# Tiles of a feed-forward group's second product placed between the next group's units

## The chip, the cores and the metric

The kernel runs on one core of a Trainium2 chip. Its engines work side by side, each through its own list of instructions: TensorE (PE; its weight loads are shown as PEld), VectorE (DVE), ScalarE (ACT), GpSimd (POOL) and SyncE (SP), which here issues the DMAs. The metric is the time of one execution on the device in microseconds (us), from several runs.

## What is computed

An encoder block of two layers on 512 tokens of width 1024. Each layer is feed-forward, token mixing, feed-forward, and a gated projection of a side input ("ple"), each followed by a layer norm. The change is in the feed-forward stage, of which there are four in all:

```python
D_MODEL, D_FF = 1024, 2816

def swiglu(x, w_in, w_out):
    gate, up = jnp.split(x @ w_in, 2, axis=-1)
    return (jax.nn.silu(gate) * up) @ w_out

x = layer_norm(ALPHA * x + 0.5 * swiglu(x, ffn_w_in[i, 0], ffn_w_out[i, 0]), ln_g[i, 0], ln_b[i, 0])
```

Inputs and weights are float32. The kernel works to more than half precision by writing each operand as a sum of two float16 numbers, `hi` and `lo`, and multiplying hi x hi, hi x lo and lo x hi: three matmuls for one (`mm3`, lines 253 to 258).

## The kernel before

The middle width of 2816 is cut into 22 columns of 128, numbered m = 0 to 21 (`MF` = 22). Column m of the gate and of the up half makes a **unit**: first product, silu, gating, and the result `h` for column m, stored as hi and lo in a tile `hT` that holds a pair of columns (`hT[m // 2]`, lines 279 to 287).

Units 0 and 1 are computed directly (lines 291 to 346). Units 2 to 21 use a Strassen-like scheme with seven products instead of eight: `load_quad` (line 430) loads two blocks of 512 KB of the first weight into a tile `f`, splits the two raw slots into hi and lo (ACT line 139, DVE line 140), and, in `rest`, makes four sums on DVE (line 453) and splits them as well, into slots 0 to 6 of a tile `wq` in the pool `ring` (three buffers; `f` has two). `begin(m)` (line 375) runs slot 0 into a PSUM bank `pA` and slot 4 into `pB`. `step(new, old)` (line 386) is a software pipeline over two units: slot 5 of the old unit, slot 2 of the new, slot 3 of the old, then silu and gating of the old, slot 1 of the new (bank `pC`), slot 6 of the new, and the copy `up` (lines 407 and 408). Each slot is twelve matmuls of 256 columns, so a unit is 84.

The second weight comes in pairs of rows: `load_rows` (line 156) loads 1 MB for columns k and k + 1 into one of three `raw` buffers and splits it (two halves on ACT line 139, two on DVE line 140) into a tile `w` of the pool `w2`, which has four buffers. `w2` also holds the weights of units 0 and 1, and the constants of the layer norm (`ln_gb`, line 169).

The columns are worked off in four **groups**, `groups = [(0, 4), (4, 10), (10, 16), (16, 22)]` (line 267), called groups 0 to 3 here. For each group (lines 410 to 428) the units run, `step(None, unit)` empties the pipeline, the group's two or three pairs of `w_out` are taken, and four **tiles** of 128 tokens follow: `out_proj` (line 459) multiplies `hT` by `w`, twice 512 output columns, each in a bank `po`, and adds them to `x` in SBUF (DVE line 472). A tile is 24 matmuls of 512 columns for group 0 and 36 for the others. In the last group each tile is followed by its layer norm.

```python
            for gi, (m0, m1) in enumerate(groups):
                unit = None
                for m in range(max(m0, 2), m1):
                    following = begin(m)
                    step(following, unit)
                    fetch(1)
                    unit = following
                step(None, unit)
                wo = weights((m1 - m0) // 2)
```

`loads` (lines 305 to 310) is the order in which weights are asked for: a group's quads, then its row pairs. `fetch(n)` keeps n of them issued ahead, `weights(n)` takes the next n.

PSUM: `acc` (line 58) hands out two banks, shared by `pC` and `po`; `bank` and `bank2` three each, for `pA` and `pB`. SBUF pools opened inside the stage (`hT`, `ring`, `f`) are given back at its end, and the next stage's pools lie on the same bytes; with `reuse_waits="tile"` a new tile waits for the old tiles that it lies on.

The order in which each engine gets its instructions isn't the order of the code alone: when the program is built, a list scheduler goes through the instructions by priority (their place in the code) and gives an engine that is free, by its estimate, the first one that is ready. At run time each engine keeps to that order and waits on semaphores.

Of the kernel before, what the change touches and what calls it, by code (L numbers as in the profile page):

```python
# [13 lines left out]
ALU = mybir.AluOpType  # L14
# [7 lines left out]
NT = S // P  # L22
DFF = 2816
MF = DFF // P
DEPTH = 2
ALPHA = (2 * DEPTH) ** 0.25
# [4 lines left out]
IWS = 1.0 / WS  # L31


class Block:
# [225 lines left out]
    def ffn(self, i, f, j, last=False):  # L260
        nc = self.nc
        w_in, w_out = self.ins["ffn_w_in"][i, f], self.ins["ffn_w_out"][i, f]
        xT, x = self.xT, self.x
# [3 lines left out]
        groups = [(0, 4), (4, 10), (10, 16), (16, MF)]  # L267
        with ExitStack() as ctx:
            pool = lambda name, bufs: ctx.enter_context(
                self.tc.tile_pool(name=name, bufs=bufs, reuse_waits="tile")  # L270
            )
            hpool = pool("hT", 4)
            self.ring = pool("ring", 3)
            self.fpool = pool("f", 2)
            hT = {}

            def gated(m, sg, ups, scale):

                if m % 2 == 0:
                    hT[m // 2] = hpool.tile([P, 2, 2, S], F16, name="hT")  # L280
                for u, part in ups:
                    nc.vector.scalar_tensor_tensor(
                        part(sg), u, scale, part(sg), op0=ALU.mult, op1=ALU.mult
                    )
                hi, lo = hT[m // 2][:, 0, m % 2], hT[m // 2][:, 1, m % 2]
                nc.scalar.activation(hi, sg, AF.Copy)  # L286
                nc.vector.tensor_tensor(lo, sg, hi, op=ALU.subtract)  # L287
# [14 lines left out]
                    )  # L302


            loads, loaded = [], []
            for m0, m1 in groups:
                loads += [lambda m=m: self.load_quad(w_in, m) for m in range(max(m0, 2), m1)]
                loads += [
                    lambda k=k: (self.load_rows(w_out, k), None) for k in range(m0, m1, 2)
                ]  # L310

            def fetch(n):
                while loads and len(loaded) < n:
                    loaded.append(loads.pop(0)())

            def weights(n):
                fetch(n)
                ws = []
                for _ in range(n):
                    w, rest = loaded.pop(0)  # L320
                    if rest:
                        rest()
                    ws.append(w)
                return ws
# [27 lines left out]
            def quarter(u, b):  # L352
                return [
                    xT[:, h, 4 * u : 4 * u + 4].rearrange("p k (a b c) -> p k a b c", a=2, b=2)[
                        :, :, :, b
                    ] for h in range(2)
                ]

            def sums(n):
                return [xS[:, h, n].rearrange("p k (a c) -> p k a c", a=2) for h in range(2)]  # L360

            def product(ps, w, n, b, first, last):
                for k in range(4):
                    self.mm3(
                        ps, [w[:, h, n, k] for h in range(2)], [b[h][:, k] for h in range(2)],
                        first and k == 0, last and k == 3, skip_group_check=True,
                    )

            def half(v, b):
                return v.rearrange("p (a b c) -> p a b c", a=2, b=2)[:, :, b]  # L370
# [4 lines left out]
            def begin(m):  # L375
                u = Unit()
                u.m, u.w = m, weights(1)[0]
                u.A = self.bank("pA", (P, 2, P))
                u.B = self.bank2("pB", (P, 2, P))
                product(u.A, u.w, 0, quarter(0, 0), True, False)  # L380
                u.sg = self.t2("sg")
                nc.scalar.activation(half(u.sg, 0), u.A, AF.Copy)
                product(u.B, u.w, 4, sums(0), True, False)
                return u

            def step(new, old):

                if old is not None:
                    product(old.A, old.w, 5, sums(3), False, True)
                if new is not None:  # L390
                    product(new.A, new.w, 2, sums(1), False, False)
                    nc.scalar.activation(half(new.sg, 1), new.A, AF.Copy)  # L392
                if old is not None:
                    product(old.B, old.w, 3, quarter(1, 1), False, True)
                    nc.vector.tensor_tensor(half(old.sg, 1), old.B, half(old.sg, 1), op=ALU.add)  # L395
                    self.ffn_end = nc.scalar.activation(old.sg, old.sg, AF.Silu, scale=IWS)
                    gated(
                        old.m, old.sg,
                        [(old.A, lambda v: half(v, 0)), (old.up, lambda v: half(v, 1))], -IWS,
                    )  # L400
                if new is not None:
                    C = self.acc("pC")[:, : 2 * P].rearrange("p (a c) -> p a c", a=2)
                    product(C, new.w, 1, quarter(1, 0), True, True)
                    nc.vector.tensor_tensor(half(new.sg, 0), C, half(new.sg, 0), op=ALU.add)
                    product(new.A, new.w, 6, sums(2), False, False)
                    new.up = self.t2("up", (P, 2, P))
                    nc.scalar.activation(new.up, new.A, AF.Copy)  # L407
                    nc.vector.tensor_tensor(new.up, new.B, new.up, op=ALU.add)

            for gi, (m0, m1) in enumerate(groups):  # L410
                unit = None
                for m in range(max(m0, 2), m1):
                    following = begin(m)
                    step(following, unit)
                    fetch(1)
                    unit = following
                step(None, unit)
                wo = weights((m1 - m0) // 2)
                if gi == len(groups) - 1:
                    gb = self.ln_consts(i, j, self.w2, tag="w")  # L420
                for t in range(NT):
                    self.out_proj(
                        t, lambda q, m: hT[(m0 + m) // 2][:, q, m % 2], wo, m1 - m0,
                        0.5 * IWS / ALPHA,
                    )
                    self.flush()
                    if gi == len(groups) - 1:
                        self.layer_norm(t, x[:, t], gb, last)

    def load_quad(self, w_in, m):  # L430

# [24 lines left out]
        split(slice(0, 2))  # L456
        return w, rest

    def out_proj(self, t, aT, wo, n, scale):

        for h in range(2):
            po = self.acc("po")
            for m in range(n):
                self.mm3(
                    po,
                    [aT(q, m)[:, t * P : (t + 1) * P] for q in range(2)],
                    [wo[m // 2][:, q, m % 2, h * 512 : (h + 1) * 512] for q in range(2)],
                    m == 0,
                    m == n - 1,
                )  # L470
            xs = self.x[:, t, h * 512 : (h + 1) * 512]
            self.nc.vector.scalar_tensor_tensor(xs, po, scale, xs, op0=ALU.mult, op1=ALU.add)  # L472


    def ple(self, i, j, last=False):
# [701 lines left out]
```

## Time and profile before

| | us |
|---|---|
| median of 3 runs | 2031.88 |
| lowest and highest | 2029.93, 2032.16 |
| the profiled execution | 2031.65 |
| its span, first to last instruction | 2029.9 |

| engine | busy us | share of the span |
|---|---|---|
| PE | 1983.4 | 98% |
| PEld | 1289.0 | 64% |
| DVE | 1523.3 | 75% |
| ACT | 874.2 | 43% |
| POOL | 64.0 | 3% |

How to read it: "L140 DVE ... wq<-f,wq" is line 140 on DVE, writing tile `wq` from `f` and `wq`. A row of the timeline gives the start, the duration, the instruction, and in brackets how long its engine sat idle before it and what it waited for. A row of the view by tile gives the durations in ns (least, median, most) and the first and last start. A row of the waits gives the total, the number and the longest wait. A row of the windows gives for each engine the busy time with the number of instructions, then the granted TensorE clock (1.00 is full), the DMA share and GB/s. Matmuls are pipelined and their ends are modelled: one of 256 columns shows some 273 ns, one of 512 some 379 ns, while the next one starts much earlier. The mean granted TensorE clock of the core was 0.997.

### The profile page before, as it was taken

What the parts mean: (1) busy time and instruction counts of PE and PEld (TensorE: products, weight loads), DVE (VectorE), ACT (ScalarE), POOL (GpSimd) and SP (SyncE); (2) the same over time, 40 slices, a digit from 0 to 9 for tenths busy, and PEclk for the clock granted to TensorE, in tenths of its full rate; (3) what the DMA queues carried; (4) which work ended last, traced back from release to release, by engine and by line L of the source; (5) the groups of instructions that cost most, each with busy time, mean ns of one, the idle gap of its engine ahead of it and who ended that gap; (6) DMA issues with size and microseconds to landing.
All of it is one profiled execution on the core that took longest, in us unless ns stands there. A gap on an engine that the chain in (4) does not pass through costs nothing.

```text
span 2029.9 us, 33679 instructions
## 1 busy us (share of the span) xinstructions
PE 1983.4 (98%) x14346; PEld 1289.0 (64%) x14346; DVE 1523.3 (75%) x2347; ACT 874.2 (43%) x1295; POOL 64.0 (3%) x84
## 2 busy tenths in 40 slices
PE   7999999999999999999999999999999999999998
PEld 5677686545545686776467686855455466776853
DVE  7995866775479986958897867577755798967686
ACT  6453352454244453543364443434533354543431
POOL 1000000100000000000000000002000000000000
PEclk9999999999999999999999999999999999999999
DMA  7533320431044443433324333222311624433221
GB/s 218 195 112 107 97 85 1 126 77 63 1 167 124 126 127 106 121 104 125 125 80 129 104 119 89 64 65 66 94 42 43 207 64 146 125 104 84 94 73 42
DMA packets 245361, 205.19 MB, mean 101 GB/s; under 512 B 20846, under 2 KB 225500, under 8 KB 245212
## 3 DMA queue, kind: packets, MB, share of 16 engines
q1 hardware_dynamic: 245212, 203.05, 32.6%
q8 instruction: 112, 1.84, 0.4%
q14 instruction: 37, 0.30, 0.0%
HBM read 200.14 MB, written 2.88 MB: 100 GB/s over the span
## 4 chain that ended last, share of the span: by engine, by line
PE 79%; DVE 12%; ACT 5%; DMA 2%; issue 1%; SPq 1%; POOL 0%; DVEq 0%; ACTq 0%
PE po L258 7%; PE po L256 7%; PE po L257 7%; PE pA L256 6%; PE pA L258 6%; PE pA L257 6%; PE pB L258 3%; PE pB L257 3%; PE pB L256 3%; DVE wq L140 3%; DVE w L140 2%; ACT w L139 2%; ACT wq L139 1%; PE pC L258 1%; PE pC L256 1%; PE pC L257 1%
## 5 line engine op out<-in xcount | busy, mean ns | idle before, releaser
L140 DVE SCALAR_TENSOR_TENSOR wq<-f,wq 128x1024 f16<-128x1024 f32 (+1 forms) x240 | 333.9, 1395 | 19.0 <-ACT wq L139 15.7
L139 ACT ACTIVATE wq<-f 128x1024 f16<-128x1024 f32 (+1 forms) x240 | 279.5, 1191 | 126.1 <-PE pB L258 83.2
L139 ACT ACTIVATE w<-raw 128x1024 f16<-128x1024 f32 (+1 forms) x196 | 193.8, 1032 | 264.6 <-PE po L258 226.3
L256 PE MATMUL po<-w,hT 128*128 128x512 f16 x704 | 266.7, 379 | 3.7 <-ACT hT L286 1.5
L256 PE MATMUL pA<-xS,wq 128*128 128x256 f16 x960 | 261.6, 272 | 6.8 <-ACT up L407 5.3
L257 PE MATMUL po<-w,hT 128*128 128x512 f16 x704 | 266.5, 379 | 0.0
L258 PE MATMUL po<-w,hT 128*128 128x512 f16 x704 | 264.3, 379 | 1.9 <-DVE hT L287 1.9
L258 PE MATMUL pA<-xS,wq 128*128 128x256 f16 x960 | 261.6, 273 | 0.0
L257 PE MATMUL pA<-xS,wq 128*128 128x256 f16 x960 | 261.6, 273 | 0.0
L140 DVE SCALAR_TENSOR_TENSOR w<-raw,w 128x1024 f16<-128x1024 f32 (+1 forms) x196 | 230.0, 1193 | 36.4 <-ACT w L139 36.4
L257 PEld LDWEIGHTS <-wq 128*128 128x128 f16 x2240 | 219.1, 98 | 42.1 <-issue 11.7
L453 DVE TENSOR_TENSOR f<-f 128x512 f32<-128x512 f32 x320 | 218.4, 686 | 28.1 <-DMA f<-in_ffn_w_in 23.0
L256 PEld LDWEIGHTS <-wq 128*128 128x128 f16 x2240 | 219.1, 98 | 30.1
L258 PEld LDWEIGHTS <-wq 128*128 128x128 f16 x2240 | 219.1, 98 | 27.5
L472 DVE SCALAR_TENSOR_TENSOR x_tok<-po,x_tok 128x512 f32<-128x512 f32 x144 | 97.5, 685 | 82.4 <-PE po L258 82.3
L256 PEld LDWEIGHTS <-hT 128*128 128x128 f16 x704 | 68.8, 98 | 85.2 <-ACT hT L286 9.9
L258 PEld LDWEIGHTS <-hT 128*128 128x128 f16 x704 | 68.0, 98 | 84.8 <-DVE hT L287 5.3
L395 DVE TENSOR_TENSOR sg<-pB,sg 128x256 f32<-128x256 f32 x80 | 33.6, 420 | 117.5 <-PE pB L258 117.5
L257 PEld LDWEIGHTS <-hT 128*128 128x128 f16 x704 | 68.9, 98 | 76.9 <-issue 1.4
L392 ACT ACTIVATE sg<-pA 128x256 f32<-128x256 f32 x80 | 30.6, 382 | 194.1 <-PE pA L258 194.1
L257 PEld LDWEIGHTS <-w 128*128 128x128 f16 x640 | 62.9, 98 | 63.1 <-issue 16.4
L256 PEld LDWEIGHTS <-w 128*128 128x128 f16 x640 | 62.7, 98 | 61.4 <-issue 6.2
(289 smaller groups left out, 3872.0 us busy)
## 6 DMA issues: line engine op xcount, KB each, us to landing
f<-in_ffn_w_in SPq DMA_DIRECT2D x160, 512.0 KB, 5.1
raw<-in_ffn_w_out SPq DMA_DIRECT2D x44, 1024.0 KB, 6.1
raw<-in_mix_w_in SPq DMA_DIRECT2D x28, 1024.0 KB, 5.3
raw<-in_mix_w_out SPq DMA_DIRECT2D x8, 1024.0 KB, 4.9
raw<-in_ple_w_gate SPq DMA_DIRECT2D x8, 1024.0 KB, 7.5
raw<-in_ffn_w_in SPq DMA_DIRECT2D x6, 1024.0 KB, 5.0
ln_gb<-in_ln_g SPq DMA_DIRECT2D x8, 512.0 KB, 3.6
ln_gb<-in_ln_b SPq DMA_DIRECT2D x8, 512.0 KB, 5.1
```

The source lines that it names most:

```text
L139: self.nc.scalar.activation(hi, raw, AF.Copy, scale=WS),
L140: self.nc.vector.scalar_tensor_tensor(lo, raw, WS, hi, op0=ALU.mult, op1=ALU.subtract),
L256: nc.tensor.matmul(ps, a[0], b[0], start=first, stop=False, **k)
L257: nc.tensor.matmul(ps, a[0], b[1], start=False, stop=False, **k)
L258: nc.tensor.matmul(ps, a[1], b[0], start=False, stop=last, **k)
L392: nc.scalar.activation(half(new.sg, 1), new.A, AF.Copy)
L395: nc.vector.tensor_tensor(half(old.sg, 1), old.B, half(old.sg, 1), op=ALU.add)
L453: nc.vector.tensor_tensor(f[:, to], f[:, a], f[:, b], op=ALU.add)
L472: self.nc.vector.scalar_tensor_tensor(xs, po, scale, xs, op0=ALU.mult, op1=ALU.add)
```

## The change

The four groups stay, but there is one loop over all units from 2 to 21, and `step` is called with `None` once, at its end. The tiles of a group are put into the loop, one behind each of four units of the next group: group 0's tiles behind units 5 to 8, group 1's behind 11 to 14, group 2's behind 17 to 20. Group 3's tiles follow the loop as before. The row pairs of the second weight are asked for one at a time: k = 0 and 2 at units 4 and 5; 4, 6 and 8 at units 9, 10 and 11; 10, 12 and 14 at units 15, 16 and 17; 16, 18 and 20 at unit 21. `hT` gets a fifth buffer. `out_proj` gets an argument `late`, used for the first tile of the last group: both halves' matmuls for all columns but the last come first, then the last column's for each half. `self.flush()` is called between the tiles of the last group only. In the kernel after, the addition to `x` stands in line 498.

```diff
-            hpool = pool("hT", 4)
+            hpool = pool("hT", 5)
...
             loads, loaded = [], []
-            for m0, m1 in groups:
-                loads += [lambda m=m: self.load_quad(w_in, m) for m in range(max(m0, 2), m1)]
-                loads += [
-                    lambda k=k: (self.load_rows(w_out, k), None) for k in range(m0, m1, 2)
-                ]
+            rows = {m: [] for m in range(2, MF + 1)}
+            for (m0, m1), first in zip(groups, (4, 9, 15, MF - 1)):
+                for n, k in enumerate(range(m0, m1, 2)):
+                    rows[min(first + n, MF - 1)].append(k)
+            for m in range(2, MF):
+                loads.append(lambda m=m: self.load_quad(w_in, m))
+                loads += [lambda k=k: (self.load_rows(w_out, k), None) for k in rows[m]]
...
-            for gi, (m0, m1) in enumerate(groups):
-                unit = None
-                for m in range(max(m0, 2), m1):
-                    following = begin(m)
-                    step(following, unit)
-                    fetch(1)
-                    unit = following
-                step(None, unit)
-                wo = weights((m1 - m0) // 2)
-                if gi == len(groups) - 1:
-                    gb = self.ln_consts(i, j, self.w2, tag="w")
-                for t in range(NT):
-                    self.out_proj(
-                        t, lambda q, m: hT[(m0 + m) // 2][:, q, m % 2], wo, m1 - m0,
-                        0.5 * IWS / ALPHA,
-                    )
-                    self.flush()
-                    if gi == len(groups) - 1:
-                        self.layer_norm(t, x[:, t], gb, last)
+            def out_tile(t, late=False):
+                m0, m1 = groups[done]
+                self.out_proj(
+                    t, lambda q, m: hT[(m0 + m) // 2][:, q, m % 2], wo[m0], m1 - m0,
+                    0.5 * IWS / ALPHA, late,
+                )
+
+            unit, done, wo, tiles = None, 0, {m0: [] for m0, _ in groups}, []
+            for m in range(2, MF):
+                following = begin(m)
+                step(following, unit)
+                unit = following
+                for k in rows[m]:
+                    group = [m0 for m0, m1 in groups if m0 <= k < m1][0]
+                    wo[group] += weights(1)
+                fetch(1)
+                if tiles:
+                    out_tile(tiles.pop(0))
+                    if not tiles:
+                        done += 1
+                elif m == groups[done][1]:
+                    tiles = list(range(NT))
+            step(None, unit)
+            gb = self.ln_consts(i, j, self.w2, tag="w")
+            for t in range(NT):
+                out_tile(t, late=t == 0)
+                self.flush()
+                self.layer_norm(t, x[:, t], gb, last)
...
-    def out_proj(self, t, aT, wo, n, scale):
-
-        for h in range(2):
-            po = self.acc("po")
-            for m in range(n):
+    def out_proj(self, t, aT, wo, n, scale, late=False):
+
+        po = [self.acc("po"), self.acc("po")] if late else [None] * 2
+
+        def part(h, ms):
+            for m in ms:
                 self.mm3(
-                    po,
+                    po[h],
                     [aT(q, m)[:, t * P : (t + 1) * P] for q in range(2)],
                     [wo[m // 2][:, q, m % 2, h * 512 : (h + 1) * 512] for q in range(2)],
                     m == 0,
                     m == n - 1,
                 )
+
+        if late:
+            for h in range(2):
+                part(h, range(n - 1))
+        for h in range(2):
+            if late:
+                part(h, [n - 1])
+            else:
+                po[h] = self.acc("po")
+                part(h, range(n))
             xs = self.x[:, t, h * 512 : (h + 1) * 512]
-            self.nc.vector.scalar_tensor_tensor(xs, po, scale, xs, op0=ALU.mult, op1=ALU.add)
+            self.nc.vector.scalar_tensor_tensor(xs, po[h], scale, xs, op0=ALU.mult, op1=ALU.add)
```

## The prediction

> **What bounds the kernel now.** First the page: how full TensorE is.
>
> ```profile
> span 2029.9 us, 33679 instructions
> ...
> PE 1983.4 (98%) x14346; PEld 1289.0 (64%) x14346; DVE 1523.3 (75%) x2347; ACT 874.2 (43%) x1295; POOL 64.0 (3%) x84
> ```
>
> TensorE is the bound, and the change leaves its matmuls as they are: it can win only the time that TensorE loses between them. The rows of neighbouring matmuls overlap, so I measure from start to start. The timeline gives the pace: L392 on ACT runs once a unit, behind the same product, and L472 on DVE once for each half tile.
>
> ```profile
> 104.73 0.38 ACT L392 ACTIVATE sg<-pA 128x256 f32<-128x256 f32 x1 [2.90 <-PE pA L258]
> ...
> 132.24 0.38 ACT L392 ACTIVATE sg<-pA 128x256 f32<-128x256 f32 x1 [2.82 <-PE pA L258]
> ```
>
> ```profile
> 164.04 0.69 DVE L472 SCALAR_TENSOR_TENSOR x_tok<-po,x_tok 128x512 f32<-128x512 f32 x1 [3.20 <-PE po L258]
> 167.93 0.69 DVE L472 SCALAR_TENSOR_TENSOR x_tok<-po,x_tok 128x512 f32<-128x512 f32 x1 [3.19 <-PE po L258]
> ```
>
> Three units take 27.51 us, so one takes 9.17 and each of its 84 matmuls 0.109. Eighteen `po` matmuls take 3.89 us, 0.216 each. Now the loss in each of the four feed-forward stages, from its first `pB` matmul to its last `po` matmul (view by tile, one window per stage; the columns to read are "first and last start").
>
> ```profile
> L256 PE MATMUL pB<-xS,wq x80: 272/273/273, 42.9 to 303.6; 128*128 128x256 f16 x80
> ...
> L258 PE MATMUL po<-w,hT x176: 379/379/390, 57.7 to 346.0; 128*128 128x512 f16 x176
> ```
>
> ```profile
> L256 PE MATMUL pB<-xS,wq x80: 272/273/273, 661.5 to 922.3; 128*128 128x256 f16 x80
> ...
> L258 PE MATMUL po<-w,hT x176: 377/379/390, 676.3 to 964.6; 128*128 128x512 f16 x176
> ```
>
> ```profile
> L256 PE MATMUL pB<-xS,wq x80: 272/273/273, 1048.5 to 1308.3; 128*128 128x256 f16 x80
> ...
> L258 PE MATMUL po<-w,hT x176: 378/379/390, 1063.4 to 1350.8; 128*128 128x512 f16 x176
> ```
>
> ```profile
> L256 PE MATMUL pB<-xS,wq x80: 272/273/273, 1663.6 to 1923.8; 128*128 128x256 f16 x80
> ...
> L258 PE MATMUL po<-w,hT x176: 377/379/390, 1678.4 to 1966.2; 128*128 128x512 f16 x176
> ```
>
> Each stretch holds 1668 unit matmuls (20 units of 84, less the first product of 12), 527 of `po` and sixteen transposes of the layer norm (line 220, put at 0.109 each, an estimate from the unit's pace): 182.1 + 113.8 + 1.7 = 297.6 us. The four took 303.1, 303.1, 302.3 and 302.6, so 5.5 + 5.5 + 4.7 + 5.0 = **20.7 us** are lost: the ceiling of what this change can win. Where, shows TensorE's timeline; the first six rows are the end of group 1 in the first stage, then the end of group 2 and of group 0.
>
> ```profile
> 137.70 0.38 PE L258 MATMUL po<-w,hT 128*128 128x512 f16 x1
> 138.37 0.27 PE L256 MATMUL pA<-xS,wq 128*128 128x256 f16 x1 [0.29 <-ACT up L407]
> ...
> 144.44 0.38 PE L257 MATMUL po<-w,hT 128*128 128x512 f16 x1
> 144.94 0.39 PE L256 MATMUL po<-w,hT 128*128 128x512 f16 x1
> ...
> 173.03 0.27 PE L258 MATMUL pB<-xS,wq 128*128 128x256 f16 x1
> 173.44 0.27 PE L256 MATMUL pA<-xS,wq 128*128 128x256 f16 x1
> ...
> 224.94 0.38 PE L258 MATMUL po<-w,hT 128*128 128x512 f16 x1
> ```
>
> ```profile
> 58.15 0.38 PE L257 MATMUL po<-w,hT 128*128 128x512 f16 x1
> 60.31 0.27 PE L256 MATMUL pA<-xS,wq 128*128 128x256 f16 x1 [1.78 <-ACT up L407]
> 60.42 0.27 PE L257 MATMUL pA<-xS,wq 128*128 128x256 f16 x1
> ```
>
> `step(None, unit)` has no next unit to lay between, so slot 5 waits for the copy `up` (0.67 - 0.22 = 0.45 us lost), the first tile waits for the last `hT` (0.50 - 0.22 = 0.28), and in the new group the second product waits for ACT (0.41 - 0.11 = 0.30). From 137.70 to 224.94 lie 87.24 us for 504 unit matmuls and 144 of `po`, 55.0 + 31.1: 1.1 us a boundary. Eight such boundaries (after groups 1 and 2, four stages) make 9.0; the other 11.7 lie in the first groups (1.94 in the one row pair above) and the last drains.
>
> **The change part by part.** *The pipeline is not emptied.* Behind each unit's slot 6 now come at most a tile and the next unit's first two products (24 matmuls, 2.6 us) before slot 5 needs `up`; `hT` of a group is finished a whole unit before its first tile. The 0.45 and 0.28, and the rest of 1.1 - 0.30, go at all eight places: 0.82 x 8 = **-6.6**. The last group still drains; the argument `late` lays 30 matmuls (6.5 us) before those that need the last `hT`.
>
> *The second weights come one pair at a time.* Same splits (two halves on ACT and two on DVE each), at other times. The 0.30 comes from them:
>
> ```profile
> 169.22 3.90 ACT L139 ACTIVATE w<-raw 128x1024 f16<-128x1024 f32 x4 [20.49 <-PE po L258]
> 173.03 0.36 ACT L382 ACTIVATE sg<-pA 128x256 f32<-128x256 f32 x1
> ```
>
> ACT sat 20.49 us behind a split that needed a `w` buffer which the tiles held, did four, and only then the copy that TensorE waited for. Buffers still come free with a group's last tile, so I let half of 0.30 x 8 stay: **-1.2** (between 0 and -2.4).
>
> *Vector time in units without a tile.* The windows compare a stretch of units with one of tiles, DVE third.
>
> ```profile
> 115.80:134.10 18.30, 18.30 (x170) 16.40 (x168) 17.90 (x27) 10.80 (x17) 0.00 (x0) 1.00 0.41 115
> 148.30:171.60 23.30, 23.30 (x110) 10.56 (x108) 11.60 (x17) 2.81 (x4) 0.00 (x0) 1.00 0.16 46
> ```
>
> DVE is 98% busy among units and 50% among tiles. Spreading the tiles evens that out, but units 4, 9, 10, 15, 16 and 21 have no tile and take on row splits, 2.3 us a pair (two halves of 1.15):
>
> ```profile
> 173.19 3.49 DVE L140 SCALAR_TENSOR_TENSOR w<-raw,w 128x1024 f16<-128x1024 f32 x3
> ```
>
> What hides them is DVE's lead on the ring:
>
> ```profile
> 124.95 0.42 DVE L395 TENSOR_TENSOR sg<-pB,sg 128x256 f32<-128x256 f32 x1
> 125.47 1.23 DVE L140 SCALAR_TENSOR_TENSOR wq<-f,wq 128x1024 f16<-128x1024 f32 x1
> ...
> 127.61 1.75 DVE L140 SCALAR_TENSOR_TENSOR wq<-f,wq 128x1536 f16<-128x1536 f32 x1
> ...
> 129.88 0.42 DVE L408 TENSOR_TENSOR up<-pB,up 128x256 f32<-128x256 f32 x1
> ```
>
> After L395 of one unit a ring buffer is free and quad m+2 is split, its large part by 129.4. The present unit m has 2.6 us left at 124.8 and unit m+1 takes 9.17, so unit m+2 needs that part at 136.5 + 1.3: a lead of 8.4 us against the 4.6 of two pairs in neighbouring units. Price 0; without the lead 2.3 a pair. What is late next is a pair due in the very unit before its tile (k = 2, 8, 14). Split early it costs nothing. Split only behind the unit's own DVE work, which ends with L408 at 130.3, 2.9 us after unit m's last product (127.4), its halves are ready 4.05 and 5.2 us into the tile; the tile wants them after 6 or 12 matmuls, at 1.3 or 2.6, and 0.65 later: 3.25 lost four times (k = 2) and 1.95 eight times, 29 in all. I take 0.4 at each of the four first groups, where DVE is fullest: **+1.6** (0 to 29).
>
> *The first groups.* Tiles 0 to 3 gave DVE 20.7 us (96 x 0.216) between units 3 and 4; now unit 4 follows at once, but the pairs k = 0, 2 (4.6 us) no longer stand ahead of its quad. I keep 2.5 of the 11.7 as Vector-bound: **-9.2** (between 0 and -11.7).
>
> *Last pairs, norm constants, SP.* k = 18, 20 and `ln_gb` get buffers only after tile 3 of group 2; SP queues the two DMAs of `ln_gb`, and whatever it has behind them, on that. Unit 21 and the closing step (9.17 + 2.6 = 11.8 us) cover 4.6 us of DVE. Price 0, up to 4.6 a stage without cover. The row DMAs move among the quads' on SP; `raw` has three buffers, so they lead. POOL gets nothing new.
>
> *A fifth `hT` buffer* shifts what the next stage's weights lie on: pair 10 instead of 8 is now last in the first buffer, and mix's first split waits for it to the stage's end.
>
> ```profile
> 343.87 1.06 ACT L139 ACTIVATE w<-raw 128x1024 f16<-128x1024 f32 x1 [4.53 <-PE po L258]
> ```
>
> It can slip from 343.87 to about 346.4. Its Vector half stood at 352.12 behind the norm, so 0 (up to 2.5 twice).
>
> ```profile
> 352.12 1.22 DVE L140 SCALAR_TENSOR_TENSOR w<-raw,w 128x1024 f16<-128x1024 f32 x1
> ```
>
> Sum: -6.6 - 1.2 - 9.2 + 1.6 = **-15.4**. The profiled execution took 2031.65 us (span 2029.9 and 1.75 around it), 0.23 under the median of 2031.88. 2031.65 - 15.4 gives **2016 us**.
>
> *A rule weighed.* After an idle stretch this trace shows the half pace:
>
> ```profile
> 372.81 0.61 PE L256 MATMUL pk<-xT,w 128*128 128x512 f16 x1 [2.11 <-DVE conv L619]
> 373.21 0.63 PE L257 MATMUL pk<-xT,w 128*128 128x512 f16 x1
> ```
>
> 0.40 instead of 0.216 behind 2.11 us; behind 1.78 us of idle the pair at 60.31 and 60.42 keeps 0.11. So no boundary costs clock today, and none is won back. The Trainium skill speaks against the change here: "TensorE: Matmul & The Clock Gate", section "A second HAM failure mode: psum-queue depth-cycling", has kernels that cycle through PSUM banks idle briefly so often that the clock keeps falling to half. By that rule each tile could start slow; the pair at 60.31 disagrees.
>
> **Rivals.** *DVE still bounds the first groups:* the 9.2 stay lost, 2025. For it: DVE is saturated there; against: the pairs step back. *The pairs come late:* two in three of them, +19 instead of +1.6, 2034, no measurable change; for it: DVE at 98%, against: the same lead. *Nothing changes:* the scheduler already mixes `po` into drains, as the row at 137.70 shows, and the same stalls move to other places: 2032. *Slower: Vector's queue is held by the tile.* Engines take work in order (ACT's 20.49 us show it).
>
> ```profile
> L453 DVE TENSOR_TENSOR f<-f 128x512 f32<-128x512 f32 x320 | 218.4, 686 | 28.1 <-DMA f<-in_ffn_w_in 23.0
> ```
>
> If L498 (L472 before), which adds a tile into `x`, is queued ahead of the next quad's four adds (4 x 0.69, the page's row above) and large split (1.75), these start when the tile ends, and the unit's second product, due 1.3 later, waits 2.7 + 1.75 - 1.3 = 3.15. Five of the 48 tiles so hit eat the gain (15.4 / 3.15), and from seven on the kernel is measurably slower (19.4 / 3.15); with a third of them hit it takes 2016 + 16 x 3.15 = 2066. Against it: the lead of 8.4. The Trainium skill says the same of the queues ("PSUM — Partial Sum Buffer", "Engine vs sequencer instructions": strict FIFO on ScalarE and VectorE); the trace agrees. *Clock halved at tile starts:* the slow stretch at 372.81 cost 0.2 a matmul; were it eight matmuls (an assumption) at each of 48 tiles, 77 us: 2093.
>
> **How the numbers follow.** Forecast (2011 to 2021): 0.60. First groups unwon (2021 to 2027.6): 0.17. Late pairs or nothing changed (within 4 us): 0.13. Held queue: 0.07; clock: 0.01. Below 2011, by the rounding of the paces: 0.02. 0.2% (4 us) is about what a measurement of this kernel can tell from no change. Faster 0.79, same 0.13, slower 0.08. Range **2010 to 2029**: everything but the slower cases and most of the unchanged.
>
> **What will show it.** Right: the stretch from first `pB` to last `po` falls from 303 to about 299 us in each stage, no `PE pA <- ACT up` wait is left, and units 9, 10, 15 and 16 run at 9.17. Wrong: `PE po <- DVE w` at a group's first tile (pairs late), `PE pB <- DVE wq` behind a tile (held queue), or a first group as long as before.

## The result, and the profile after

The kernel after takes **2059.92 us** (median of 4 runs, 2057.84 to 2060.34), the kernel before 2031.65 us, measured beside it (4 runs, 2029.93 to 2032.16): a ratio of 1.0139, 95% interval 1.0121 to 1.0156. It is slower by 1.4%, far outside my range. The profiled execution took 2057.84 us. First the page, then the view by tile for the first two feed-forward stages (least, median and longest duration in ns, then first and last start), to set beside the rows of before.

```profile
span 2056.1 us, 33663 instructions
...
PE 1989.0 (97%) x14346; PEld 1295.2 (63%) x14346; DVE 1525.2 (74%) x2347; ACT 874.3 (43%) x1295; POOL 63.9 (3%) x84
```

```profile
L256 PE MATMUL pB<-xS,wq x80: 272/273/273, 42.3 to 308.0; 128*128 128x256 f16 x80
...
L258 PE MATMUL po<-w,hT x176: 378/379/379, 77.7 to 350.4; 128*128 128x512 f16 x176
```

```profile
L256 PE MATMUL pB<-xS,wq x80: 272/273/273, 663.2 to 928.9; 128*128 128x256 f16 x80
...
L258 PE MATMUL po<-w,hT x176: 377/379/634, 696.8 to 971.4; 128*128 128x512 f16 x176
```

The counts of instructions in the last row are those of before, and each stretch from first `pB` to last `po` has grown: 308.1, 308.1, 305.2 and 307.2 us where before had 303.2, 303.2, 302.2 and 302.6. That is +17.4 us where I expected -15.4. A second loss stands in a stage that the prediction never looked at, the per-layer one, here from the first to the last `pgate` matmul. The first fence is before, the second after; in each, the first execution of the stage and then the second.

```profile
L256 PE MATMUL pgate<-w,xT x64: 379/379/379, 965.7 to 1019.7; 128*128 128x512 f16 x64
...
L258 PE MATMUL pgate<-w,xT x64: 379/379/379, 1967.7 to 2018.0; 128*128 128x512 f16 x64
```

```profile
L256 PE MATMUL pgate<-w,xT x64: 377/379/379, 972.7 to 1033.5; 128*128 128x512 f16 x64
...
L258 PE MATMUL pgate<-w,xT x64: 377/379/379, 1990.9 to 2044.2; 128*128 128x512 f16 x64
```

I call these the gate stretches: 54.4 and 50.7 us before, 61.3 and 55.2 after, +11.3. All the rest of the span is 2.6 us shorter. 17.4 + 11.3 - 2.6 gives the 26.2 by which the span grew (2029.9 to 2056.1; the terms are rounded).

**The first loss: VectorE stands before an add.** The groups of the waits of after (total, number, longest), TensorE's first:

```profile
PE pA L256 <- ACT up L410: 13.1, 11, 2.7
PE po L256 <- DVE sg L407: 12.9, 11, 2.6
```

```profile
DVE f L467 <- DMA f<-in_ffn_w_in: 79.7, 32, 6.8
```

The same three in before:

```profile
PE pA L256 <- ACT up L407: 5.3, 11, 1.8
PE po L256 <- DVE sg L404: 0.7, 1, 0.7
```

```profile
DVE f L453 <- DMA f<-in_ffn_w_in: 23.0, 13, 2.4
```

One stall shows how they hang together; the timeline of VectorE in the first stage, then SP's and TensorE's rows of the same moments:

```profile
100.67 1.23 DVE L140 SCALAR_TENSOR_TENSOR wq<-f,wq 128x1024 f16<-128x1024 f32 x1
101.82 2.14 DVE L467 TENSOR_TENSOR f<-f 128x512 f32<-128x512 f32 x3
103.88 0.42 DVE L398 TENSOR_TENSOR sg<-pB,sg 128x256 f32<-128x256 f32 x1
107.89 0.69 DVE L467 TENSOR_TENSOR f<-f 128x512 f32<-128x512 f32 x1 [3.60 <-DMA f<-in_ffn_w_in]
108.50 1.22 DVE L140 SCALAR_TENSOR_TENSOR wq<-f,wq 128x1024 f16<-128x1024 f32 x1
109.63 0.42 DVE L282 SCALAR_TENSOR_TENSOR sg<-pA,sg 128x256 f32<-128x256 f32 x1
109.97 0.42 DVE L282 SCALAR_TENSOR_TENSOR sg<-up,sg 128x256 f32<-128x256 f32 x1
110.30 0.42 DVE L407 TENSOR_TENSOR sg<-pC,sg 128x256 f32<-128x256 f32 x1
```

```profile
101.93 0.37 SPq L453 DMA_DIRECT2D f<-in_ffn_w_in  x1
102.34 0.58 SPq L454 DMA_DIRECT2D f<-in_ffn_w_in  x1
```

```profile
108.58 0.38 PE L258 MATMUL po<-w,hT 128*128 128x512 f16 x1
110.77 0.38 PE L256 MATMUL po<-w,hT 128*128 128x512 f16 x1 [1.81 <-DVE sg L407]
```

The split at 100.67 ends at 101.90 and gives an `f` buffer back; SP issues the next quad's loads into it at 101.93. The first add of that quad runs at 107.89, 6 us later (the page gives 5.1 as the median from issue to landing of these loads). But it stands in VectorE's queue ahead of `L282` and `L407`, the evacuations of the present unit. The last `pC` product starts at 104.8, so they could have run soon after 105; they wait with it. `L407` ends at 110.72 and gives `po`'s second half its bank: TensorE starts at 110.77, after 2.19 us where 0.22 is the pace. VectorE was not short of time here, it stood still.

The costliest stall of each stage has another mixture. It stands at the end of group 1, where slot 5 of unit 9 waits for `up` (at 143.47 in the first stage), and it costs 2.9 us in each of the four stages. VectorE, again in the first stage:

```profile
136.44 2.87 DVE L467 TENSOR_TENSOR f<-f 128x512 f32<-128x512 f32 x4 [0.76 <-DMA f<-in_ffn_w_in]
139.23 0.42 DVE L398 TENSOR_TENSOR sg<-pB,sg 128x256 f32<-128x256 f32 x1
```

The last product into that `pB` starts at 135.27, and the row pairs' splits on VectorE end at 135.69. `L398` could have run then; it runs 3.5 us later, of which 0.8 is the wait for the DMA and 2.8 are the adds themselves. Silu and the copy `up` on ScalarE follow it. So the place of the adds in the queue costs TensorE time even when they hardly wait.

**The second loss: ScalarE splits the gate weights late.** ScalarE's timeline at the end of the second feed-forward stage, before and then after (`w<-raw` behind the last `hT` are halves of the per-layer stage's weight pairs):

```profile
929.63 1.05 ACT L139 ACTIVATE w<-raw 128x1024 f16<-128x1024 f32 x1
933.61 1.99 ACT L139 ACTIVATE w<-raw 128x1024 f16<-128x1024 f32 x2
```

```profile
941.26 0.63 ACT L286 ACTIVATE hT<-sg 128x512 f16<-128x512 f32 x1 [0.88 <-DVE sg L282]
954.92 1.08 ACT L223 ACTIVATE xT<-ps_t 128x512 f16<-128x512 f32 x2 [13.03 <-PE ps_t L220]
963.56 1.08 ACT L223 ACTIVATE xT<-ps_t 128x512 f16<-128x512 f32 x2 [7.56 <-PE ps_t L220]
964.53 1.06 ACT L139 ACTIVATE w<-raw 128x1024 f16<-128x1024 f32 x1
```

The first half was split at 929.63 before and at 964.53 after, with 20 us of idle ScalarE ahead of it, and it did not wait for anything itself: it came next in a queue whose head waited for transposes. When the gate's matmuls begin at 972.7, TensorE waits for the weights (`PE pgate <- DVE w`, 3.1 us in 5 waits). With its waits on the layer norm and on evacuations, which stand in VectorE's queue among the late splits, TensorE waits 9.7 us in the two gate stretches; before it was 0.7.

### The profile page after: what moved, and what is told of

The parts are those of the page before. It is cut to its first block, busy times and chain, and to the rows that moved or that the text cites. A ratio compares the mean times of both kernels' runs of the same rounds, so it can differ in the third digit from the quotient of the medians.

```text
span 2056.1 us, 33663 instructions
## 1 busy us (share of the span) xinstructions
PE 1989.0 (97%) x14346; PEld 1295.2 (63%) x14346; DVE 1525.2 (74%) x2347; ACT 874.3 (43%) x1295; POOL 63.9 (3%) x84
## 4 chain that ended last, share of the span: by engine, by line
PE 38%; DVE 8%; DMA 2%; ACT 2%; issue 1%; POOL 0%; SPq 0%; DVEq 0%; ACTq 0%
PE po L256 4%; PE po L257 4%; PE po L258 4%; PE pA L256 2%; PE pA L257 2%; PE pA L258 2%; DMA f<-in_ffn_w_in 2%; DVE f L467 2%; DVE w L140 1%; DVE wq L140 1%; PE pB L257 1%; PE pB L258 1%; PE pB L256 1%; ACT w L139 1%; PE pgate L256 1%; PE pgate L258 1%
## 5 line engine op out<-in xcount | busy, mean ns | idle before, releaser
L467 DVE TENSOR_TENSOR f<-f 128x512 f32<-128x512 f32 x320 | 218.9, 687 | 85.5 <-DMA f<-in_ffn_w_in 79.7
L256 PE MATMUL pA<-xS,wq 128*128 128x256 f16 x960 | 263.0, 274 | 14.6 <-ACT up L410 13.1
L395 ACT ACTIVATE sg<-pA 128x256 f32<-128x256 f32 x80 | 30.7, 383 | 209.5 <-PE pA L258 209.5
L385 ACT ACTIVATE sg<-pA 128x256 f32<-128x256 f32 x80 | 30.1, 377 | 203.1 <-PE pA L258 203.1
L223 ACT ACTIVATE xT<-ps_t 128x512 f16<-128x512 f32 x64 | 35.7, 595 | 169.9 <-PE ps_t L220 169.6
L398 DVE TENSOR_TENSOR sg<-pB,sg 128x256 f32<-128x256 f32 x80 | 33.6, 420 | 94.5 <-PE pB L258 94.5
```

What stands on the lines that cost most here:

```text
L223: nc.scalar.activation(hi, ps, AF.Copy),
L256: nc.tensor.matmul(ps, a[0], b[0], start=first, stop=False, **k)
L467: nc.vector.tensor_tensor(f[:, to], f[:, a], f[:, b], op=ALU.add)
```

## The experiments

Each was timed beside the kernel before (2032.5 to 2033.0 us there). "Stretches" are the four feed-forward ones in their order, "gate" the two of the per-layer stage, all from first to last start in the profile.

| kernel | median us | ratio to before, 95% interval | stretches | gate |
|---|---|---|---|---|
| before | 2031.65 | | 303.2 303.2 302.2 302.6 | 54.4 50.7 |
| after | 2059.92 | 1.0139 (1.0121 to 1.0156) | 308.1 308.1 305.2 307.2 | 61.3 55.2 |
| e1 adds' order | 2031.92 | 0.9994 (0.9985 to 1.0004) | 301.7 299.2 299.4 299.2 | 63.1 55.3 |
| e2 the same, in before | 2032.08 | 0.9996 (0.9987 to 1.0006) | 302.3 303.0 302.4 302.7 | 54.4 50.7 |
| e3 `ln_gb` behind the weights | 2060.43 | 1.0137 (1.0122 to 1.0152) | 308.0 308.6 307.1 308.2 | 59.3 55.5 |
| e4 group 0 in place | 2034.95 | 1.0012 (1.0002 to 1.0021) | 301.4 300.5 300.2 300.7 | 62.7 55.6 |
| e5 before, five `hT` | 2045.63 | 1.0066 (1.0051 to 1.0081) | 303.9 303.9 302.1 302.7 | 61.2 55.3 |
| e6 e1 and `hT` last | 2019.85 | 0.9939 (0.9924 to 0.9953) | 302.8 299.2 301.1 299.2 | 54.5 50.4 |
| e7 `hT` last alone | 2047.45 | 1.0082 (1.0065 to 1.0099) | 309.2 307.7 306.9 307.9 | 54.5 50.4 |
| e8 `pC` in other banks | 2059.12 | 1.0133 (1.0117 to 1.0148) | 306.8 309.7 305.3 307.9 | 61.3 56.1 |
| e9 third `f` | 2045.91 | 1.0064 (1.0049 to 1.0079) | 301.1 303.2 305.6 301.8 | 62.8 55.4 |
| e10 e9 and `hT` last | 2033.29 | 1.0003 (0.9994 to 1.0013) | 302.8 304.4 303.5 305.4 | 54.5 50.4 |
| e11 e6 without `late` | 2018.99 | 0.9932 (0.9918 to 0.9947) | 301.8 299.1 300.8 299.1 | 54.4 50.7 |
| e12 before, `hT` last | 2031.23 | 0.9999 (0.9989 to 1.0008) | 304.6 302.9 303.9 302.6 | 54.4 50.7 |

### The feed-forward stretches: is it the queue or the work?

**e1.** The call to `self.after` fixes the order of two instructions on an engine when the kernel is built; it adds no wait. `split` now returns its last instruction on VectorE; nothing else is changed.

```diff
             for to, a, b in ((6, 0, 4), (4, 4, 5), (2, 0, 4), (3, 1, 2)):
-                nc.vector.tensor_tensor(f[:, to], f[:, a], f[:, b], op=ALU.add)
-            split(slice(4, 7), slice(2, 4))
+                add = nc.vector.tensor_tensor(f[:, to], f[:, a], f[:, b], op=ALU.add)
+                if to == 6 and self.split_end is not None:
+                    self.after(add, self.split_end)
+            self.split_end = split(slice(4, 7), slice(2, 4))
```

> The kernel after, with one order added on VectorE: the four adds of a quad stand behind the last split of the quad before. Theory A (VectorE's queue is held by adds that wait for their own DMA, with the evacuations of pB, pA, up and pC behind them): the waits of the adds on f<-in_ffn_w_in fall from 79.7 us to under 25, the PE waits po <- DVE sg (12.9) and pA <- ACT up (13.1) go, each feed-forward stretch falls from about 307 to 299 to 302 us, and the kernel takes 2030 to 2042. Rival R (VectorE has more work in units 2 to 9 than time, whatever its order): the stalls only move to other VectorE operations, each stretch stays within 2 us of 307, 2052 to 2068.

2031.92 us: 28 us come back by the order alone. Of TensorE's two waits, the groups of lines and operations keep 0.8 and 2.9 us (behind the bar: idle before and what ended it), and the adds stand idle for 5.2 us in all:

```profile
L256 PE MATMUL po<-w,hT 128*128 128x512 f16 x704 | 266.8, 379 | 0.8 <-DVE sg L407 0.8
L256 PE MATMUL pA<-xS,wq 128*128 128x256 f16 x960 | 261.7, 273 | 4.0 <-ACT up L410 2.9 <-ACT sg L385 1.0
...
L468 DVE TENSOR_TENSOR f<-f 128x512 f32<-128x512 f32 x320 | 220.5, 689 | 5.2
```

VectorE does the same 220 us of adds. So the work was never too much for units 2 to 9; it stood in the wrong place.

**e2.** The same edit in the kernel before.

> The kernel before with the same order added, as a control. Theory A: its adds wait 23.0 us for DMA, mostly in time in which VectorE had nothing else to do, and only 5.3 us of PE waits on up stand in its stretches: within 4 us of 2031.65. Were the order a gain or a loss of its own, whatever the tiles do, it would show here: 2010 to 2025, or over 2040.

2032.08 us. The order is no gain of its own; it matters only where the tiles lie between the units.

**e4.** Only group 0's tiles are taken out of the loop's later turns, and its pairs asked for a unit earlier.

```diff
-            for (m0, m1), first in zip(groups, (4, 9, 15, MF - 1)):
+            for (m0, m1), first in zip(groups, (3, 9, 15, MF - 1)):
...
                 elif m == groups[done][1]:
                     tiles = list(range(NT))
+                    while done == 0:
+                        out_tile(tiles.pop(0))
+                        if not tiles:
+                            done = 1
```

> The kernel after, with the four tiles of group 0 placed together behind unit 4's products (the pipeline not emptied) and its two pairs one unit earlier; groups 1 and 2 stay spread. Theory A and rival R both say that the stalls of units 6 to 9 come from the first group: the stretches fall from 307 to 299 to 303 us, 2030 to 2044. Were the spreading of groups 1 and 2 at fault as well, the stretches stay above 304 us, over 2048.

2034.95 us, stretches of 300 to 301. Here no order is given, and the adds wait half as long:

```profile
DVE f L471 <- DMA f<-in_ffn_w_in: 37.3, 20, 2.3
```

So it is the first group that brings VectorE's queue out of step, and with it in place groups 1 and 2 can be spread without harm. That the 20.7 us of its tiles, in one piece between two units, are what lets loads and adds catch up is my reading; the run also moves the group's two pairs by a unit, and does not tell the two apart.

**e8.** A rival for `po`'s stall: `pC` and `po` share two banks.

```diff
-                    C = self.acc("pC")[:, : 2 * P].rearrange("p (a c) -> p a c", a=2)
+                    C = self.bank2("pC", (P, 2, P))
```

> The kernel after with pC in pB's three banks instead of the two it shares with po. Rival S (the stall of po comes from sharing two banks with pC): po <- DVE sg (12.9 us) goes and the stretches fall by 3 us or more each, 2040 to 2050. Theory A (VectorE is held by the adds, and every evacuation behind them is late): the stall moves to pB's banks or to up, the adds still wait 70 us or more, the stretches change by under 1.5 us each, 2053 to 2068.

2059.12 us. The stall moved with the banks, from `po <- DVE sg L407` to `pB <- DVE sg L398`:

```profile
PE pA L256 <- ACT up L410: 12.2, 14, 2.3
PE pB L256 <- DVE sg L398: 8.1, 4, 2.1
```

The shared banks are where the delay was seen, not where it arose.

**e9** takes the wait away in another way: a third `f` buffer, so that loads start a quad earlier. To fit, a buffer has five slots, and the sums of slots 2 and 3 go to one of their own.

```diff
-            self.fpool = pool("f", 2)
+            self.fpool, self.spool = pool("f", 3), pool("s", 1)
...
-        f = self.fpool.tile([P, 7, 4, P], F32, name="f")
+        f = self.fpool.tile([P, 5, 4, P], F32, name="f")
...
+            s = self.spool.tile([P, 2, 4, P], F32, name="s")
+            for to, a, b in (
+                (f[:, 4], f[:, 0], f[:, 2]), (f[:, 2], f[:, 2], f[:, 3]),
+                (s[:, 0], f[:, 0], f[:, 2]), (s[:, 1], f[:, 1], s[:, 0]),
+            ):
+                nc.vector.tensor_tensor(to, a, b, op=ALU.add)
+            split((slice(4, 7), f[:, 2:5]), (slice(2, 4), s))
```

> The kernel after with three f buffers of five slots each in place of two of seven (the two sums of slots 2 and 3 go to a buffer of their own), so that a quad's loads start a quad earlier; no order is added. Theory A (the wait of the adds for their DMA is the cause, in whatever way it is removed): the adds' DMA waits fall from 79.7 to under 25 us, the feed-forward stretches to 299 to 303, the gate stretches stay at 61 and 55, 2029 to 2037. Rival (the order of e1 helped in another way, the wait itself costs little): the stretches stay above 305, 2050 to 2062.

This missed on both counts. 2045.91 us, with stretches of 301 to 306, half way between the two theories; and the waits of the adds did not fall at all:

```profile
DVE f L471 <- DMA f<-in_ffn_w_in: 80.7, 48, 3.4
```

They are more and shorter (80.7 / 48 = 1.7 us on average against 79.7 / 32 = 2.5, the longest 3.4 instead of 6.8). As I read it, the order fixed at build uses another buffer to move the adds forward again, up to loads that have not landed; that is argued, not shown, and the one buffer of `s`, which every quad now shares, is a change of its own. What the run does show is that the total of the waits says little: it is the same as in after, and 14 us come back. (Before had 23.0 us, and e2, which orders its adds, gains nothing.) What counts is whether an evacuation that TensorE needs stands behind the adds.

### The gate stretches: which queue, and why?

**e3.** SP's queue offered the first suspect: it stands 38.2 us before `ln_gb` of the per-layer stage, with the third weight pair's load behind it.

```diff
-            gb = self.ln_consts(i, j, pool)
+            gb = self.ln_consts(i, j, pool, after=self.loaded, both=True)
```

(`both` puts the load of each half behind the last weight pair; elsewhere the first half alone, as it was.)

> The kernel after, with the two ln_gb loads of the per-layer stage put behind its last weight pair on SP's queue. Theory B (SP's queue stands 38.2 us on that ln_gb, and the third to fifth weight pairs behind it): they are issued 30 us earlier, the two gate stretches fall from 61.3 and 55.2 us to near the 54.4 and 50.7 of before, 8 to 11 us less, 2049 to 2052. Rival (the pairs wait for buffers or for VectorE and ScalarE anyway): the SP wait goes, the gate stretches stay, within 3 us of 2060.

The theory fell: 2060.43 us. SP's waits between 880 and 1000 us show why:

```profile
SPq L159 <- DVE rs L187: 48.1, 2, 44.5
```

SP now stands 44.5 us before the weight load itself (line 159), whose `raw` buffer is given back by the late splits. SP followed ScalarE, not the other way round.

**e5.** The kernel before with one number changed.

```diff
-            hpool = pool("hT", 4)
+            hpool = pool("hT", 5)
```

> The kernel before with five hT buffers in place of four and nothing else. Theory C (the fifth buffer moves the other pools up by 4 KB, so that the per-layer stage's first weight pair lies over hT's pool, and the order fixed at build puts its splits behind the last tile): the two gate stretches grow from 54.4 and 50.7 us to about 61 and 55, the feed-forward stretches stay at 303, 2041 to 2046. Rival D (the gate stretches are long because the last pairs k = 18, 20 hold w2 and raw buffers until tile 3 of group 2): nothing changes, within 3 us of 2032.

2045.63 us, and the gate stretches are those of after to 0.1 us (61.2 and 55.3): 12.6 us for a buffer that the kernel before never needed. Pools lie one above the other, so 4 KB more of `hT` push `ring` up. In the per-layer stage 16 KB of its own tiles lie below the gate weights: as much as four `hT` buffers. So the first gate weight (8 KB), which before lay over `ring` alone, now lies over the topmost `hT` slot too.

**e6.** e1, and `hT` opened above the other two pools; **e7**, the same without e1's order.

```diff
-            hpool = pool("hT", 5)
             self.ring = pool("ring", 3)
             self.fpool = pool("f", 2)
+            hpool = pool("hT", 5)
```

> e1 with the hT pool opened after ring and f, so that it lies above them. Theory C: the gate stretches fall back from 63.1 and 55.3 us to 54 to 56 and 50 to 52, the feed-forward stretches stay at 299 to 302, 2017 to 2023, faster than both kernels. Rival D: the gate stretches stay, 2029 to 2035.

> The kernel after with hT's pool last and without the order of e1. If the two losses are separate, the feed-forward stretches stay near 307 and the gate stretches fall to 54 to 56 and 50 to 52: 2046 to 2051. If the layout also had to do with the stretches, under 2040.

2019.85 and 2047.45 us: the gate stretches are back at 54.5 and 50.4 in both, and the two losses add up: the order takes 28.0 us from after, the layout 12.5, both together 40.1. e6 splits the first gate half before the tiles again; ScalarE's rows of e6:

```profile
922.28 0.63 ACT L286 ACTIVATE hT<-sg 128x512 f16<-128x512 f32 x1 [0.88 <-DVE sg L282]
923.21 1.05 ACT L139 ACTIVATE w<-raw 128x1024 f16<-128x1024 f32 x1
```

**e12.** The control: the kernel before with its four `hT` buffers above the others.

> The kernel before with its four hT buffers opened after ring and f, as a control for e6: how much of e6's gain is the layout alone. Theory C (before, no weight of the per-layer stage lies over hT in a way that matters): the gate stretches stay at 54 and 51, within 3 us of 2032. If the layout itself is the gain, 2019 to 2026.

2031.23 us, the gate stretches at 54.4 and 50.7. The layout is no gain in itself, it only takes back what the fifth buffer cost.

**e10.** e9 with `hT` last.

> e9 with hT's pool last. Theories A and C together: stretches 299 to 303 and gate stretches 54 and 50, 2015 to 2023. If the order of e1 is needed as well, 2026 to 2045.

2033.29 us: e1's order is needed as well.

**e11.** e6, with `out_tile(t, late=t == 0)` made `out_tile(t)`.

> e6 without the split of a group's last first tile (late), so that tile 0 of the last group runs all of its first half before its second. If the last pair (k = 20) is ready in time, which I priced at nothing, within 2 us of 2020; if late hides it, up to 2.3 us a stage more, 2022 to 2029.

2018.99 us against 2019.85, within what can be told apart. `late` is worth nothing here. e6 and e11 are the fastest kernels, each 0.6 to 0.7% faster than before.

## Why the prediction was wrong, by its own steps

| step | predicted us | measured |
|---|---|---|
| pipeline not emptied, no held-up copies behind row splits | -6.6 - 1.2 | -9.1 in e1; +7.0 in after |
| first groups (with the last drains) and late pairs | -9.2 + 1.6 | -3.3 in e1; +9.8 in after |
| fifth `hT` buffer | 0 | +11.3 in the gate stretches |

The measured numbers of the first two rows are the time lost between TensorE's matmuls in all four stretches: start to start, less 0.109 for a matmul of 256 columns or a transpose and 0.216 for one of 512. The first row is the middle of a stretch, from the end of unit 9's slot 4 to the last `pB`, which holds both boundaries of a stage; the second row is what lies before and behind it. In the middle before loses 9.7, after 16.6 and e1 0.5; outside it 12.0, 21.8 and 8.7. (e1's loss is 12.4 us smaller than before's and its stretches are 11.8 shorter, because 0.6 us of other matmuls now lie inside them.) Of after's 16.6, the stall at unit 9 is 11.5 in the four stages, and the half pace behind two of them (see the last section) another 3.1.

- **The boundaries were right.** Of the 9.0 us that I counted there, 7.8 were to go; 9.1 of 9.7 went as soon as VectorE's adds stood in order. e2 keeps its 9.7: it is the tiles' new place that wins them.
- **"What hides them is DVE's lead on the ring ... Price 0" failed.** I followed the splits' lead over TensorE and took each VectorE instruction to run once its buffer was free. I never followed `f`: two buffers, a load that takes 5.1 us from issue and starts only when the quad before last is wholly split, and adds whose place in the queue is fixed at build. With the first group's tiles spread, the adds stood ahead of the evacuations and often ahead of their data. The term put at 0 measured 29 us: the loss of after's stretches falls from 38.4 to 9.2 when e1 gives the adds their order.
- **"The first groups", -9.2, was too large as well.** With the 1.6 for pairs I forecast -7.6; with the adds in order it is -3.3. Of the 8.7 us still lost, 4 lie in the first stage.
- **"Pairs late", +1.6: none.** No wait of `po` on a weight is left among after's waits of a microsecond or more.
- **The rival "held queue", at a chance of 0.07, was the right kind of fault** with the wrong holder. I asked whether a tile's addition would stand ahead of the next quad's adds (3.15 us each); it was the adds that stood ahead of the unit's evacuations. The rule of the Trainium skill on the queues that is cited there ("PSUM — Partial Sum Buffer", "Engine vs sequencer instructions") is what the rows at 103.88 and 107.89 show: the evacuations wait behind the add. My reason against the rival, the lead of 8.4 us, was counted for the splits only.
- **"A fifth `hT` buffer", 0, failed.** I worked out what lies on `hT` in the stage behind the first stretch and stopped. The stage behind the second and the fourth was not looked at, and that is where the bytes moved under a weight that ScalarE splits early. Mix, which I did price, became 2.6 us shorter in the first layer and 0.2 longer in the second, from the last `po` of one stretch to the first `pB` of the next.
- **"SP, price 0":** SP did stand 19.2 and 38.2 us before the two `ln_gb` loads at the second stage's end (the stage's own, then the per-layer stage's). e3 shows that taking the second away wins nothing; the first was not tried alone.

Signs: the stretch falls to 299 in three of e1's four stages, as I wrote for the change, and it grew in after. `PE pA <- ACT up` was to vanish and went from 5.3 to 13.1 us. Of the three wrong signs that I named, the two waits of TensorE on `w` and `wq` did not come. The third, a first group as long as before, was outdone: up to unit 9's slot 4, after loses 21.3 us in the four stages and before 10.8.

What stays open: an order given at build lets the scheduler place other instructions anew as well, and how much of e1's 28 us comes from such moves no run tells apart. Open is also why the build puts the gate's first split behind the transposes once its weight overlaps `hT`. The last group's three pairs do not lie in that slot, and the trace shows no wait of the split itself; that the build orders it by the pool and not by the slot is only argued. That the overlap is the condition is shown by e5, e6 and e12.

## What to carry to other kernels

Where instructions run in a fixed order on each engine, follow every input of what you spread out, its loads too: an instruction that is placed ahead of its data, or ahead of an evacuation that is due, holds everything that is queued behind it. The sign is a cheap evacuation that runs microseconds after its product is there, whether its engine idled or worked in between. A pool that grows moves all that lies above it, so look at every later stage that reuses those bytes. When a large rearrangement loses, look for the part that was right: here one order and one line of layout turn 2060 into 2020 us.

## What the chip showed beside

After 1.81 us of idle (at 110.77) TensorE kept its pace; after 2.69 us it ran fourteen matmuls at half pace. TensorE's timeline of after:

```profile
143.47 0.37 PE L256 MATMUL pA<-xS,wq 128*128 128x256 f16 x1 [2.69 <-ACT up L410]
143.64 0.42 PE L257 MATMUL pA<-xS,wq 128*128 128x256 f16 x1
...
146.41 0.33 PE L258 MATMUL pA<-xS,wq 128*128 128x256 f16 x1
146.59 0.27 PE L256 MATMUL pA<-xS,wq 128*128 128x256 f16 x1
```

From 143.64 to 146.41 thirteen steps take 2.77 us, 0.213 each instead of 0.109, and the granted clock of these moments is 0.50: the stall cost 1.4 us more than its own length. But the length alone does not decide. Six stalls of after's stretches lose 2.4 us or more. Three of them, with 2.23, 2.69 and 2.73 us of idle (at 716, 143 and 764), each went with one piece of 3.4 us at the clock 0.50 that starts within half a microsecond of the stall's end; the other three, with 2.59, 2.71 and 2.71 (at 1749, 1162 and 1782), with none. What makes the difference no run here shows. The mean granted clock of the core fell to 0.995 from 0.997. The Trainium skill ("TensorE: Matmul & The Clock Gate", section "HAM oscillation — how this bites in real kernels") gives about 3.4 us as the idle time to stay under; the row above disagrees, after 2.69 us the pace was halved. The Trainium skill's other rule (same page, section "A second HAM failure mode: psum-queue depth-cycling"), that short idling between banks makes the clock swing, which I had weighed as a rival, does not show in after: the stall of 1.81 us cost only itself.
